# Laying a scan group's pieces inside the next group's projections in a hybrid attention and state-space layer

## The chip, the cores and the metric

The kernel runs on one NeuronCore of one Trainium2 chip. The metric is the device time of one execution in microseconds (us); lower is better. TensorE does the matrix products and transposes, VectorE (DVE in the profile), ScalarE (ACT) and GpSimd (POOL) the elementwise work, and SyncE (SP) issues all DMAs in one queue, in order.

## The reference, cut to what matters

One layer over 512 latent tokens and 256 context tokens, width 2048. The normalised input goes through one combined projection `w_in`, whose columns feed a windowed attention (q, k, v, a gate) and a bidirectional state-space scan in 4 groups of 4 heads (x, B, C, two step sizes dt, a gate z). The scan of a group, for each direction and in chunks of 128 tokens:

```python
    a_cs = jnp.cumsum(a_t, axis=-1)
    cb = jnp.einsum('bclgn,bcsgn->bgcls', cc, bc)
    wts = cb[:, :, None] * jnp.exp(segsum(a_t))
    y_diag = jnp.einsum('bgrcls,bcsgrp->bclgrp', wts, xdt)
    states = jnp.einsum('bclgn,bgrcl,bclgrp->bcgrpn', bc, decay_states, xdt)
    ...
    y_off = jnp.einsum('bclgn,bcgrpn,bgrcl->bclgrp', cc, prev, jnp.exp(a_cs))
    return (y_diag + y_off).reshape(b, l, g, r, p), final
```

x, B and C first pass a depthwise convolution of width 3 and a silu. The scan of the latent tokens starts from the context's final state; k, x and B are needed for context tokens too, q, C and the gates for latent tokens only. Both halves are then gated, normalised and sent through one output projection.

## The kernel before, in words

Every fp32 product of a projection is done as three products of a split operand (high and low part of the weight, `wh` and `wl`, and of the input, `xh` and `xl`, or `ch` and `cl` for the context). A **unit** is 128 projection columns: `load_unit` brings its weights in two DMAs (`wr`, 512 KB each, two buffers), ScalarE makes `wh` and VectorE makes `wl` in four quarters, and `proj` runs over 16 k blocks. For each it issues three products of 512 columns into the PSUM tile `pj` (L321 to L323) and, for units that the context needs, three products of 256 columns into `pjc` (L325 to L327). With every quarter `gate_step` (L274) adds one block of the residual gate's row in VectorE (L290), with a DMA `wg` each; after every 16 blocks it sums over the partitions in two TensorE instructions `gp` (L293).

The SSD stage takes 16 units, four for each group (two of x, one B, one C), and `ssd_group` (L474) writes them out group by group:

- four projections, each followed by `conv_silu` (L459), which reads the PSUM tiles three times each (L465, L466, L468);
- transposes of x and B into token layout (`xtp` L496, `btp` L503), copied by ScalarE into `xtok` and `btok`;
- the chunk states: `stc`, then three serial steps of `stx` for both directions, each with VectorE work (`xw`, `stt`) before and after;
- the product `cbp` of C and B, copied into `cb`;
- for each of two head pairs (`pr`): the state term `z` (L548); for each of four rows (2 heads, 2 directions) the **decay**: a broadcast DMA of the running sums into a tile `df` (L562, four buffers), exponentials on ScalarE, masks (L566), scaling (L573, L575) and the product with `cb` on VectorE; then the products `yps` (L586) of the pair's two decay matrices with `xtok`, the tile `yt` (L591) and three GpSimd instructions (sum of `ec`, `yt`, and the product into `yT`).

After the four groups the SSD pool is closed and the attention pool opens in the same room (`sst.close()`, L606; `at`, L610). The two key units (k0, k1) are projected in a loop there, each followed by its rotation `rope_apply` (L623, with the table `rp` loaded by a DMA at L620) into that pool. Then come `finish_half` of the scan's output, and four attention blocks whose query units (q0, q1 for the first) and gate units are projected in between.

The order on each engine is not the order of the text: a list scheduler, with a cost model of its own, takes the ready instruction of the best priority, which is the place in the text, moved forward in `high_priority` blocks. So products of the next units already fill gaps in a group's chain. What runs on the chip is then a fixed order for each engine, and a wait in it holds up all that is behind. PSUM has eight banks: 3 of tag `mm` (for `pj` and `pjc`), 2 `sa` (`z`), 2 `tp` (transposes, states, `cbp`, `gp`) and 1 `pv` (`yps`).

Of the kernel before, what the change touches and what calls it, by code (L numbers as in the profile page):

```python
# [14 lines left out]
P = 128  # L15
D = 2048
KT = 16
# [26 lines left out]
def emit(tc, xin, ctxT, wmod, wgate, bgate, wz, wvd, wu, wo, fng, vecs, cst, rope, out, dbg=None):  # L44
# [18 lines left out]
    with es:  # L63
# [24 lines left out]
        # persistent activations: transposed normalised inputs in two exact parts  # L88
# [27 lines left out]
        def rms_rows(o, acc, n, tag):  # L116
            """1 / rms of every token, on all partitions, from the sums of squares per partition."""
# [13 lines left out]
        def load_latent():  # L131
            """Latent tokens: transposed as they come, in column blocks; 1 / rms of every token on all partitions."""
# [44 lines left out]
        # silu of the two modulation vectors, zero-padded to one column group  # L177
# [95 lines left out]

        def gate_step(ld):  # L274
            """One k block of 512 gate columns: products per partition, summed over partitions after the last."""
# [3 lines left out]
            n, k = divmod(i, KT)  # L279
            if k == 0:  # L280
                ga = wp.tile([P, 512], F32, tag="ga", name=f"ga_{n}", bufs=1)
# [9 lines left out]
            if k == KT - 1:  # L291
                gp = bank("tp", f"gp_{n}", shape=(1, 512))
                mm(gp, ones[:, 0:1], ga, True, True)  # L293
                nc.scalar.activation(ga[0:1, :], gp, AF.Copy)
                nc.sync.dma_start(grow[:, n * 512:(n + 1) * 512], ga[0:1, :])

# [1 line left out]
        def load_unit(u, ctxp=False):  # L298
            """Yields (k, hi, lo) weight blocks [128, 128] of unit u."""
# [16 lines left out]
        def proj(u, with_ctx):  # L316
            a = bank("mm", f"pj_{u}")
            b = bank("mm", f"pjc_{u}", shape=(P, CT)) if with_ctx else None
            for k, wh, wl in load_unit(u):
                s0, s1 = k == 0, k == KT - 1  # L320
                mm(a, wh, xh[k], s0, False)  # L321
                mm(a, wh, xl[k], False, False)
                mm(a, wl, xh[k], False, s1)  # L323
                if with_ctx:
                    mm(b, wh, ch[k], s0, False)  # L325
                    mm(b, wh, cl[k], False, False)
                    mm(b, wl, ch[k], False, s1)  # L327
            return a, b

# [80 lines left out]
        # dt: softplus(u) = max(u,0) + log1p(exp(-|u|)), log1p(e) = 2 atanh(e / (2 + e))  # L410
        fl = [P, 192]
        uu = dtt.rearrange("p a b c -> p (a b c)")
        ue = w2("ue", "sm", 4, fl)
        us = w2("us", "sm", 4, fl)
        u2 = w2("u2", "sm", 4, fl)
        acc = w2("acc", "sm", 4, fl)
# [12 lines left out]
        da = w2("da", "sm", 4, fl)  # L429
# [13 lines left out]
        dd = w2("dd", "sm", 4, fl)  # L443
# [6 lines left out]
        csx = w2("csx", "sm", 4, [P, NT, 2, 16])  # L450
# [8 lines left out]
        def conv_silu(pa, pb, ci, o):  # L459
            """Depthwise conv of width 3 and silu: pa [128, n] in PSUM -> o in SBUF."""  # L460
# [13 lines left out]
        def ssd_group(g, units):  # L474
            ux0, ux1, ub, uc = units
            xs = []
            for i, u in enumerate((ux0, ux1)):
# [532 lines left out]
```

## Time and profile before

| what | value |
|---|---|
| device time, three executions | 1060.71, 1056.16 and 1057.65 us, median 1057.65 |
| profiled execution, span from first to last instruction | 1054.8 us |
| TensorE (PE) busy | 1009.6 us, 96% |
| TensorE weight loads (PEld) busy | 818.7 us, 78% |
| VectorE (DVE) busy | 722.0 us, 68% |
| ScalarE (ACT) busy | 494.6 us, 47% |
| GpSimd (POOL) busy | 173.5 us, 16% |
| mean granted TensorE clock | 0.989 of full speed |

The span is 2.85 us below the median of the three times. A busy share is the time in which an engine had an instruction open; for TensorE, whose matmuls overlap, a busy engine is not one at its peak.

### The profile page before, as it was taken

The numbers are of one execution on the slowest core, as the hardware profiler recorded it, in microseconds if no ns is written. First come the engines' busy times: TensorE is split into PE (matmuls) and PEld (weight loads), VectorE is DVE, ScalarE is ACT, GpSimd is POOL, SyncE is SP. The second block draws the span as 40 slices with busy tenths as digits, with TensorE's granted clock in tenths as the row PEclk, the third lists the DMA queues.
The fourth block names the chain that finished last, engine by engine and source line by source line (L and its number), as shares of the span: only waits on it lengthen the run. The fifth ranks groups of instructions, "written<-read, shape, count | busy, mean of one in ns | idle before, by whom it ended". The sixth has DMA issues, their size and how long they took to land.

```text
span 1054.8 us, 15524 instructions
## 1 busy us (share of the span) xinstructions
PE 1009.6 (96%) x5682; PEld 818.7 (78%) x5682; DVE 722.0 (68%) x1474; ACT 494.6 (47%) x1064; POOL 173.5 (16%) x120
## 2 busy tenths in 40 slices
PE   5999999999999989989989999999999998999996
PEld 4677789788778868868868777777777777888885
DVE  4332378585875985885889888788798866333765
ACT  6222275263352453263345567666666655333333
POOL 1232200000210110110037100000000008744220
PEclk9999999999999999989999999999999999999998
DMA  9999963354244244444331211112111135442304
GB/s 333 385 347 348 343 212 95 110 165 147 70 120 145 92 149 125 112 120 139 120 107 56 84 61 42 59 40 80 41 40 61 61 99 221 151 167 91 100 33 160
DMA packets 50845, 143.25 MB, mean 136 GB/s; under 512 B 5544, under 2 KB 5928, under 8 KB 50512
## 3 DMA queue, kind: packets, MB, share of 16 engines
q1 hardware_dynamic: 50768, 142.25, 40.5%
q8 instruction: 45, 0.74, 0.3%
q14 instruction: 32, 0.26, 0.1%
HBM read 137.96 MB, written 4.27 MB: 135 GB/s over the span
## 4 chain that ended last, share of the span: by engine, by line
PE 61%; DVE 12%; DMA 5%; ACT 3%; issue 3%; POOL 1%; SPq 0%; ACTq 0%; DVEq 0%; POOLq 0%
PE pj L49 25%; PE o L49 14%; PE pjc L49 5%; PE pv L49 3%; PE ptp L756 3%; PE sl L49 3%; DMA wg<-in_wgate_dram 2%; PE vps L49 2%; DVE df L566 2%; DVE wl L55 2%; DMA df<-csd 2%; PE sc L49 2%; DVE ga L290 1%; DVE df L575 1%; PE stx L49 1%
## 5 line engine op out<-in xcount | busy, mean ns | idle before, releaser
L49 PE MATMUL pj<-xh,wh 128*128 128x512 f32 x560 | 225.5, 403 | 0.0
L49 PE MATMUL pj<-xl,wh 128*128 128x512 f32 x560 | 224.6, 401 | 0.0
L49 PE MATMUL pj<-xh,wl 128*128 128x512 f32 x560 | 224.0, 400 | 0.0
L308 ACT ACTIVATE wh<-wr 128x512 fp32r<-128x512 f32 x140 | 87.9, 630 | 137.5 <-PE pjc L49 66.2
L49 PEld LDWEIGHTS pj<-xh,wl 128*128 128x128 f32 x560 | 105.7, 189 | 21.3 <-issue 0.9
L55 DVE TENSOR_TENSOR wl<-wr,wh 128x512 fp32r<-128x512 f32 x140 | 103.5, 742 | 24.9 <-ACT wh L308 21.0
L49 PEld LDWEIGHTS pj<-xl,wh 128*128 128x128 f32 x560 | 106.4, 190 | 15.1 <-issue 1.9
L49 PEld LDWEIGHTS pj<-xh,wh 128*128 128x128 f32 x560 | 106.5, 190 | 13.9 <-issue 1.0
L55 DVE TENSOR_TENSOR wol<-wo,woh 128x512 fp32r<-128x512 f32 x56 | 53.3, 968 | 63.6 <-ACT woh L846 57.3
L290 DVE SCALAR_TENSOR_TENSOR ga<-wg,sc,ga 128x512 f32<-128x512 f32 x64 | 50.8, 794 | 49.2 <-DMA wg<-in_wgate_dram 48.1
L55 POOL TENSOR_TENSOR ec<-ec,ec 128x512 f32<-128x512 f32 x8 | 11.2, 1397 | 349.2 <-DVE ec L55 328.9
L846 ACT ACTIVATE woh<-wo 128x512 fp32r<-128x512 f32 x56 | 34.8, 630 | 70.8 <-PE o L49 62.3
L55 POOL TENSOR_TENSOR hacc<-hacc,hsq 128x512 f32<-128x512 f32 x14 | 20.4, 1454 | 288.7 <-ACT hsq L654 286.3
L49 PE MATMUL pjc<-chq,wh 128*128 128x256 f32 x224 | 65.2, 291 | 2.1 <-DVE xs L468 2.1
L49 PE MATMUL pjc<-clq,wh 128*128 128x256 f32 x224 | 64.4, 288 | 0.0
L49 PE MATMUL pjc<-chq,wl 128*128 128x256 f32 x224 | 63.7, 284 | 0.0
L760 ACT ACTIVATE ph<-ptp 128x512 fp32r<-128x512 f32 x72 | 41.1, 597 | 28.2 <-PE ptp L756 26.8
L49 PE MATMUL o<-woh,hsh 128*128 128x512 f32 x128 | 50.9, 397 | 3.1 <-ACT part L865 3.1
L55 DVE TENSOR_TENSOR pl<-ptp,ph 128x512 fp32r<-128x512 f32 x72 | 48.4, 683 | 7.8 <-ACT ph L760 7.4
L566 DVE SCALAR_TENSOR_TENSOR df<-df,cs,cs_sb 128x128 f32<-128x128 f32 x128 | 48.3, 433 | 4.6 <-ACT ec L563 4.5
L49 PEld LDWEIGHTS pjc<-chq,wh 128*128 128x128 f32 x224 | 42.2, 189 | 11.5 <-ACT ec L563 1.6
L55 POOL TENSOR_TENSOR wsl<-wsr,wsh 128x896 fp32r<-128x896 f32 x16 | 33.9, 2116 | 101.0 <-ACT wsh L231 95.7
(282 smaller groups left out, 2341.8 us busy)
## 6 DMA issues: line engine op xcount, KB each, us to landing
wr<-in_wu_dram SPq DMA_DIRECT2D x70, 512.0 KB, 3.9
wm<-in_wmod_dram SPq DMA_DIRECT2D x64, 512.0 KB, 7.5
wg<-in_wgate_dram SPq DMA_DIRECT2D x64, 256.0 KB, 2.6
wo<-in_wo_dram SPq DMA_DIRECT2D x32, 512.0 KB, 4.5
df<-csd SPq DMA_DIRECT2D x32, 256.0 KB, 4.1
wsr<-in_wz_dram SPq DMA_DIRECT2D x16, 448.0 KB, 6.6
wr_v<-in_wvd_dram SPq DMA_DIRECT2D x16, 288.0 KB, 2.9
xt<-in_xin_dram SPq DMA_DIRECT2D x8, 512.0 KB, 7.5
```

Source lines behind the costliest of these rows:

```text
L49: return nc.tensor.matmul(o, l, r, start=start, stop=stop)
L55: eng.tensor_tensor(out=o, in0=a, in1=b, op=op)
L290: geng.scalar_tensor_tensor(out=ga, in0=wg, scalar=sc0[:, k:k + 1], in1=ga, op0=ALU.mult, op1=ALU.add)
L308: nc.scalar.activation(wh, rr, AF.Copy)
L566: nc.vector.scalar_tensor_tensor(out=df[:, cc], in0=bc[:, cc], scalar=cs[:, d, c, r:r + 1], in1=mF if d == 0 else mB, op0=ALU.subtract, op ...
L575: nc.vector.scalar_tensor_tensor(out=dx[0][:, cc], in0=df[:, cc], scalar=dtt[:, d, c, r:r + 1], in1=dx[0][:, cc], op0=ALU.mult, op1=ALU.add)
L756: nc.tensor.transpose(tp[:, i * P:(i + 1) * P], pt[i][:, n * P:(n + 1) * P], ident)
L760: nc.scalar.activation(ph, tp, AF.Copy)
L846: nc.scalar.activation(wh, wr[:, i, :], AF.Copy)
```

## The change

Four things are edited.

1. `ssd_group` is taken apart into functions (`stream`, `tokens`, `states`, `decay`, `state_term`, `back`), and `proj` gets an argument `mid`, a table from a k block to a function that is written out ahead of that block. The pieces of group g are so written inside the four units of group g + 1; those of the last group inside k0 and k1, which move ahead of the close of the SSD pool and keep their PSUM tiles until the rotation. `pjc` of k1 goes to a `tp` bank.
2. The three context products of a k block are no longer issued right behind its latent products, but four blocks together at the end of each quarter.
3. The `gp` sum of the gate's row is issued three gate steps later (after the last row, behind the last group), with a second buffer for `ga`.
4. Room: the x and B tiles get four slots handed out by name in place of three of one tag, and the small tiles of the step sizes share the `df` buffers.

```diff
+        def gate_sum():
+            while gpend:
+                n = gpend.pop()
...
+                mm(gp, ones[:, 0:1], ga, True, True)
...
+            if k == 3:
+                gate_sum()
...
-        def proj(u, with_ctx):
+        def proj(u, with_ctx, mid=(), btag="mm"):
             a = bank("mm", f"pj_{u}")
-            b = bank("mm", f"pjc_{u}", shape=(P, CT)) if with_ctx else None
+            b = bank(btag, f"pjc_{u}", shape=(P, CT)) if with_ctx else None
+            late = []
             for k, wh, wl in load_unit(u):
                 s0, s1 = k == 0, k == KT - 1
+                if k in mid:
+                    mid[k]()
                 mm(a, wh, xh[k], s0, False)
                 mm(a, wh, xl[k], False, False)
                 mm(a, wl, xh[k], False, s1)
                 if with_ctx:
-                    mm(b, wh, ch[k], s0, False)
-                    mm(b, wh, cl[k], False, False)
-                    mm(b, wl, ch[k], False, s1)
+                    late.append((k, wh, wl))
+                    if k % 4 == 3:
+                        for kk, h, l in late:
+                            mm(b, h, ch[kk], kk == 0, False)
+                            mm(b, h, cl[kk], False, False)
+                            mm(b, l, ch[kk], False, kk == KT - 1)
+                        late = []
...
+        def small(name, n=192):
+            return w2(name, "df", DF)[:, 0:n]
...
+        slots = ["xs0", "xs1", "xs2", "xs3"]
+        G = [{} for _ in range(4)]
+
+        def stream(g, i, mid=()):
...
+            a, b = proj(u, i < 3, mid)
...
+            conv_silu(a, b, (2 * g, 2 * g + 1, 8 + g, 12 + g)[i], o)
...
+        def tokens(g):
...
+            cbp = bank("tp", f"cbp_{g}")
...
+            slots.append(G[g]["slot2"])
+
+        def states(g):
...
+        def decay(g, pr):
...
+        def state_term(g, pr, tags=("sa", "sa")):
...
+            for d in range(2):
+                tt(nc.vector, ecs[d], zs[d], ecs[d], ALU.mult)
+            tt(nc.gpsimd, ecs[0], ecs[0], ecs[1], ALU.add)
+
+        def back(g, pr):
...
+            yps = bank("pv", f"yps_{tix}")
...
+        for i in range(4):
+            stream(0, i)
+        kps = []
         for g in range(4):
-            ssd_group(g, [U0 + 4 * g + i for i in range(4)])
...
+            if g < 3:
+                stream(g + 1, 0, {8: tok})
+                sta()
+                stream(g + 1, 1, {4: dec[0], 8: ste[0]})
+                stream(g + 1, 2, {8: do(bck[0], dec[1], ste[1])})
+                stream(g + 1, 3, {8: bck[1]})
+            else:
+                kps.append(proj(U0 + 16, True, {8: tok, 12: sta}))
+                dec[0]()
+                kps.append(proj(U0 + 17, True, {4: do(ste[0], dec[1]), 10: bck[0], 14: ste[1]}, "tp"))
+                bck[1]()
+        gate_sum()
...
-            a, b = proj(U0 + 16 + i, True)
+            a, b = kps[i]
```

`tokens` holds `cbp`, `xtp` and `btp` with their copies; `states` the `stc` and `stx` steps; `decay(g, pr)` the four rows of one head pair; `state_term` the `z` products and the three instructions on `ec`; `back` the `yps` products and what follows them. Their bodies are those of `ssd_group`; the order within is as before except that `cbp` comes first.

## Rows read from the trace of the kernel before

**Rows 1.** Busy time by stage; times in us from the span's start, instructions in brackets.
```profile
core 0: us, PE busy (x) PEld busy (x) DVE busy (x) ACT busy (x) POOL busy (x), PEclk, DMA share, GB/s
195.30:260.30 65.00, 62.63 (x344) 53.67 (x343) 45.83 (x99) 28.15 (x53) 0.00 (x0) 1.00 0.49 153
260.30:343.30 83.00, 78.82 (x450) 66.31 (x449) 61.39 (x125) 35.55 (x69) 8.46 (x7) 0.98 0.37 113
343.30:426.50 83.20, 78.34 (x458) 66.06 (x457) 63.96 (x129) 36.55 (x70) 8.53 (x7) 1.00 0.41 124
426.50:509.50 83.00, 78.45 (x441) 65.47 (x440) 63.78 (x130) 34.57 (x68) 8.58 (x7) 0.96 0.44 127
509.50:564.30 54.80, 50.81 (x305) 41.87 (x304) 47.34 (x87) 23.45 (x44) 14.46 (x10) 0.97 0.29 90
592.00:866.00 274.00, 273.47 (x1452) 215.03 (x1451) 225.43 (x545) 170.15 (x446) 0.00 (x0) 1.00 0.17 54
```

**Rows 2.** Waits of TensorE, 183 to 592: who waited for whom, us, times, longest.
```profile
PE yps L49 <- DVE df L55: 13.6, 4, 4.0
PE pjc L49 <- DVE xs L468: 2.1, 2, 1.2
PE gp L49 <- DVE ga L290: 1.9, 1, 1.9
```

**Rows 3.** Timeline of TensorE in a unit: start, us, instruction.
```profile
299.37 0.39 PE L49 MATMUL pj<-xl,wh 128*128 128x512 f32 x1
299.60 0.40 PE L49 MATMUL pj<-xh,wl 128*128 128x512 f32 x1
...
301.38 0.28 PE L49 MATMUL pjc<-clq,wh 128*128 128x256 f32 x1
301.50 0.28 PE L49 MATMUL pjc<-chq,wl 128*128 128x256 f32 x1
```

**Rows 4.** Timeline of TensorE in the first group's own products.
```profile
265.95 1.13 PE L49 MATMUL stc<-xw,btok 128*128 128x256 f32 x4
...
273.42 2.33 PE L49 MATMUL z<-cT,stt 128*128 128x128 f32 x18
275.50 0.48 PE L49 MATMUL pj<-xl,wh 128*128 128x512 f32 x1
...
276.15 1.09 PE L49 MATMUL yps<-df,xtok 128*64 128x128 f32 x16
277.17 0.38 PE L49 MATMUL z<-cT,stt 128*128 128x128 f32 x1
```

**Rows 5.** Timeline of TensorE at the last group's end; idle before in brackets.
```profile
526.71 1.09 PE L49 MATMUL yps<-df,xtok 128*64 128x128 f32 x16
...
543.43 1.45 PE L49 MATMUL yps<-df,xtok 128*64 128x128 f32 x16 [3.95 <-DVE df L55]
...
545.41 0.63 PE L49 MATMUL pj<-xh,wh 128*128 128x512 f32 x1
...
564.31 0.39 PE L49 MATMUL pj<-xh,wh 128*128 128x512 f32 x1
```

**Rows 6.** Timeline of VectorE and GpSimd: masks of the decay, and one GpSimd instruction.
```profile
285.70 1.14 DVE L566 SCALAR_TENSOR_TENSOR df<-df,cs,cs_sb 128x128 f32<-128x128 f32 x4
...
445.88 3.32 DVE L566 SCALAR_TENSOR_TENSOR df<-df,cs,cs_sb 128x128 f32<-128x128 f32 x4
...
446.13 1.29 POOL L55 TENSOR_TENSOR yt<-yt,ec 128x512 f32<-128x512 f32 x1 [1.38 <-DVE yt L591]
```

**Rows 7.** DMA issues, 195 to 560: count, KB each, median us to landing.
```profile
df<-csd SPq DMA_DIRECT2D x32, 256.0 KB, 4.1
rp<-in_rope_dram SPq DMA_DIRECT2D x1, 512.0 KB, 5.1
```

**Rows 8.** Timeline of VectorE: the rotation's two reads of k0's PSUM tile.
```profile
553.64 0.69 DVE L55 TENSOR_TENSOR kr<-pj,rp 128x512 f32<-128x512 f32 x1 [0.41 <-DMA rp<-in_rope_dram]
...
555.30 0.74 DVE L625 STREAM_SHUFFLE krt<-pj 128x512 f32<-128x512 f32 x1
```

More of the change, by code (lines that the diff above doesn't have):

```diff
@@ L531, in ssd_group @@
                     tt(nc.vector, stt_[d][:, nx, :], stt_[d][:, nx, :], sp_, ALU.add)
-            cbp = bank("tp", f"cbp_{g}")
+            G[g]["stt"] = stt_
+        def decay(g, pr):
+            cb = G[g]["cb"]
+            tix = 2 * g + pr
+            ecs = [w2(f"ec_{tix}_{d}", "ec", 3) for d in range(2)]
+            dm = []
+            for hh in range(2):
+                r = tix * 2 + hh
+                hr = slice(hh * 64, hh * 64 + 64)
+                dx = []
+                for d in range(2):
+                    df = w2(f"df_{r}_{d}", "df", DF)
+                    bc = df
+                    with tc.high_priority(HB):
+                        nc.sync.dma_start(df, csd[d * 16 + r].partition_broadcast(P))
+                    nc.scalar.activation(ecs[d][hr], bc[hr], AF.Exp)
+                    for c in range(NT):
+                        cc = slice(c * P, (c + 1) * P)
+                        nc.vector.scalar_tensor_tensor(
+                            out=df[:, cc], in0=bc[:, cc], scalar=cs[:, d, c, r:r + 1],
+                            in1=mF if d == 0 else mB, op0=ALU.subtract, op1=ALU.min)
+                    nc.scalar.activation(df, df, AF.Exp)
+                    for c in range(NT):
+                        cc = slice(c * P, (c + 1) * P)
+                        if d == 0:
+                            nc.scalar.activation(df[:, cc], df[:, cc], AF.Copy, scale=dtt[:, d, c, r:r + 1])
+                        else:
+                            nc.vector.scalar_tensor_tensor(out=dx[0][:, cc], in0=df[:, cc],
+                                                           scalar=dtt[:, d, c, r:r + 1], in1=dx[0][:, cc],
+                                                           op0=ALU.mult, op1=ALU.add)
+                    dx.append(df)
+                tt(nc.vector, dx[0], dx[0], cb, ALU.mult)
+                dm.append(dx[0])
+            G[g]["dec", pr] = dm, ecs
@@ new lines, in state_term @@
+        def state_term(g, pr, tags=("sa", "sa")):
+            stt_, cT = G[g]["stt"], G[g][3]
+            ecs = G[g]["dec", pr][1]
+            tix = 2 * g + pr
+            zs = []
+            for d in range(2):
+                z = bank(tags[d], f"z_{tix}_{d}")
+                for c in range(NT):
+                    cc = slice(c * P, (c + 1) * P)
+                    mm(z[:, cc], stt_[d][:, c, pr * P:(pr + 1) * P], cT[:, cc], True, True)
+                zs.append(z)
+            for d in range(2):
+                tt(nc.vector, ecs[d], zs[d], ecs[d], ALU.mult)
+            tt(nc.gpsimd, ecs[0], ecs[0], ecs[1], ALU.add)
@@ L597, in emit @@
[L597 to L599 removed]
+                for hh in (1, 0):
+                    hl = pr * 2 + hh
+                    mmo(yps[hh * 64:hh * 64 + 64, cc], xtok[:, c, hl * HD:hl * HD + HD], dm[hh][:, cc], True, True)
+            yt = w2(f"yt_{tix}", "cve", 1)
+            nc.vector.scalar_tensor_tensor(out=yt, in0=xs[:, 0:S], scalar=dskh[:, tix:tix + 1], in1=yps,
+                                           op0=ALU.mult, op1=ALU.add)
@@ new lines, in back, with do @@
+            tt(nc.gpsimd, yt, yt, ec, ALU.add)
+            tt(nc.gpsimd, yT[tix], yT[tix], yt, ALU.mult)
+            slots.append(G[g][f"slot{pr}"])
+        for i in range(4):
+            stream(0, i)
+        kps = []
+        for g in range(4):
+            def do(*fs):
+                return lambda: [f() for f in fs]
+            tok, sta = (lambda: tokens(g)), (lambda: states(g))
+            dec = [lambda pr=pr: decay(g, pr) for pr in range(2)]
+            ste = [lambda pr=pr: state_term(g, pr) for pr in range(2)]
+            bck = [lambda pr=pr: back(g, pr) for pr in range(2)]
+            if g < 3:
[4 more added lines that the diff above has]
+                stream(g + 1, 3, {8: bck[1]})
+            else:
+                kps.append(proj(U0 + 16, True, {8: tok, 12: sta}))
+                dec[0]()
+                kps.append(proj(U0 + 17, True, {4: do(ste[0], dec[1]), 10: bck[0], 14: ste[1]}, "tp"))
+                bck[1]()
```

116 lines of the change are left out of this document (33 added, 83 removed).

## The prediction

> **What bounds the kernel now.** I read the stages first [rows 1], then what TensorE waits for in the SSD stage [rows 2], then the timeline around the longest of these waits [rows 5] and around the instructions that end it [rows 6].
>
> TensorE is the bound. In the attention stage it is busy for 273.5 of 274 us, so nothing can be won there, only lost. The SSD stage is looser: group 0's units take 65.0 us with 2.4 idle, the three stretches that each hold one group's tail and the next group's units take 83.0, 83.2 and 83.0 us with 4.2, 4.9 and 4.5 idle (length less PE busy), and the last, with k0, k1 and group 3's tail, 54.8 us with 4.0 idle [rows 1]. VectorE is busy for 61 to 64 us of a period (74 to 77%): loaded, but not the bound.
>
> The idle time has an owner. Of what TensorE waits for there, 13.6 us in four waits is `yps` on the `df` tile, one in each group; 2.1 us is `pjc` on the convolution that still reads its PSUM bank, and 1.9 us is one `gp` on its last gate step [rows 2]. The four are the second head pair's. In the last group `yps` of pair 0 starts at 526.71 and that of pair 1 at 543.43, 16.7 us later, with TensorE idle for the last 3.95 [rows 5]: the decay of pair 1 takes longer than the products that lie under it. Behind that wait the next 512-column product takes 0.63 us instead of 0.39 [rows 5, 3], and the granted clock of the stretches with such waits is 0.98, 1.00, 0.96 and 0.97, where the others have 1.00 [rows 1]: part of the time at 1.2 instead of 2.4 GHz.
>
> **How much there is to win.** Back to back, a 512-column product is issued every 0.23 us (299.37 to 299.60) and a 256-column one every 0.12 [rows 3]. A group's four units have 192 and 144 of them: 192 x 0.23 + 144 x 0.12 = 44.2 + 17.3 = 61.5 us. The group's own products, counted from the loops (an fp32 product shows as two instructions): 58 of `z`, `cbp`, `xtp`, `btp` at (275.50 - 273.42) / 18 = 0.116 each make 6.7 us; 32 `yps` at (277.17 - 276.15) / 16 = 0.064 make 2.0; 20 `stc` and `stx` at no more than 1.13 / 4 = 0.28 make 5.6 [rows 4]; two `gp`, taken as two 512-column products each, 1.0. Sum 15.3. So a period needs 61.5 + 15.3 = 76.8 us of TensorE and takes (83.0 + 83.2 + 83.0) / 3 = 83.1: 6.3 us are lost, of which 4.5 is idle and 1.8 the slow clock and the mixing of short and long products. Over three periods at most 18.8 us can come back. The last stretch needs 96 x 0.23 + 96 x 0.12 + 15.3 = 48.9 us and takes 54.8 [rows 1]: 5.9 lost.
>
> **The change part by part.** Nothing is removed or added in work: the same products, DMAs (`df` 32, `rp` 1 [rows 7]), ScalarE and VectorE instructions. What moves is where they stand.
>
> *Group tails inside the next units, three periods.* Between the last product of C's unit and the pieces that need its convolution lie 8 k blocks, 8 x (0.69 + 0.36) = 8.4 us. Pair 0's decay now has all of unit 1 from block 4 on and half of unit 2: 12 x 1.05 + 8.4 = 21 us, more than the 16.7 of a decay between two `yps`; its wait, zero before, stays zero. Between the two `back` pieces lie half of unit 2 (8.4), the `z` products (16 x 0.116 = 1.9) and half of unit 3, which has no context products (8 x 0.69 = 5.5): 15.8 us against a chain of 16.7. So of each 3.4 us (13.6 / 4) about 0.9 stays; with a wait that short I expect no slow clock. Of the 1.8 us of mixing I leave 0.4, since the state steps still alternate with unit 1's products. Left over 1.3 a period, so won 3 x (6.3 - 1.3) = 15.0 us. Bounds: nothing (the chain grows by as much as its cover) to 18.8.
>
> *A rule against it.* The chain of 16.7 us is partly GpSimd's doing: four masks of the decay took 3.32 us while GpSimd worked on `yt`, and 1.14 us elsewhere [rows 6]. In the change `decay` of pair 1 still stands right behind `back` of pair 0, which issues those GpSimd instructions, so I keep the longer duration; by the shorter one the chain would be 2.2 us less, and the 0.9 left would go too, 2.7 us in three periods. The Trainium skill ("SBUF — State Buffer", section "Who interferes with whom") says why: a VectorE instruction with two SBUF inputs and a GpSimd one that reads SBUF exclude each other through a shared port. The trace agrees (3.32 against 1.14 us).
>
> *Context products a quarter behind.* Their rate is the same in a batch of 12 as elsewhere (0.12 us [rows 3]); cost nothing. A unit's `pj` is now complete 12 x 0.12 = 1.4 us before the unit ends, so the convolution starts that much earlier, and the next unit needs its second bank only after 12 latent products, 2.8 us. The two waits of at most 1.2 us [rows 2] go: 1.2 of the 2.1 lies in the periods and is in the sum above; the other 0.9, in group 0, is extra. If VectorE is late with the convolution they come back, 2.1 at most.
>
> *The `gp` sum three gate steps later.* Its 1.9 us wait [rows 2] lies in a period, already counted. *Shared small tiles, four slots, second `ga`*: nothing; the step sizes are done before the first `df` is wanted, and each slot is freed at least half a unit ahead of its next writer. Cover gone: a wait of the convolution for one `yt`.
>
> *SP's queue.* The `df` DMAs, some of which wait for a buffer that `yps` frees, move past weight loads; the weights queue behind them. TensorE has no wait on `wl` in this stage [rows 2], since a weight buffer holds half a unit (8.4 us). Hidden as long as an SP wait stays below that; each us beyond is a us on TensorE.
>
> *The last group.* Before, k1 lay behind group 3's end and filled the time until the rotations had freed PSUM banks: after `yps` came the rest of k0 and all of k1, and q0 began at 564.31 without a wait [rows 5]. Now k0 and k1 are used up as cover. Two waits can appear. First, pair 1's decay starts 6 k blocks (6.3 us) before `back` of pair 0, whose `df` buffers it needs for its last row; behind that `back` lie 6 x 1.05 + 1.9 = 8.2 us of products. The chain of 16.7 less 6.3 is 10.4: a wait of 2.2 us. It is 0 if only the last row is left (its DMA 4.1 and masks 1.14 fit [rows 6, 7]), 8.5 if the whole chain is. Second, k0's two tiles and k1's hold all three `mm` banks when q0 wants one. The first to go is k0's context tile, one ScalarE copy; I take 1.5 us, which the last `gp` partly covers. If that copy's room is not free, q0 waits for the rotation: the table's DMA of 5.1 us [rows 7] and two reads of 0.69 and 0.74 [rows 8], 6.5 us. With the same 2 us of slow clock and mixing as before: 48.9 + 2.2 + 1.5 + 2.0 = 54.6 against 54.8. So 0.2 won, which I count as nothing; bounds +5.9 and 48.9 + 8.5 + 6.5 + 2.0 = 65.9, a loss of 11.
>
> **Sum.** 15.0 + 0.9 + 0 = 15.9 us off the span of 1054.8, so 1038.9. The median of the runs is 2.85 above the span, so 1041.7; I say 1042.
>
> **Rivals.**
> - *All of it comes back*: no wait in any period, and the last stretch at its floor. 18.8 + 2.4 (group 0's idle) + 5.9 = 27 us: 1031. For it: the cover is only 0.9 us short of the chain, and the masks' short duration would close that. Against: the last stretch has less cover, not more.
> - *The chain stays the pace*: VectorE has the same 61 to 64 us to do in a shorter period, in order; decays that start later than before, behind convolutions and states, arrive as late as now. Each period keeps 3.4 us of wait and its clock, and only `pjc` (2.1), `gp` (1.9) and some mixing come back, some 5 us: 1053, no change to speak of. For it: the chain's hand-overs between DMA, ScalarE and VectorE are untouched. Against: pair 0 never waited, with a cover like the one pair 1 now gets.
> - *Slower: the end is bare.* Place: between k1's last product and q0's first. TensorE has nothing else to issue there, so wait for the chain (8.5) and for the rotation (6.5) are both paid, 11 us lost; behind it VectorE has both rotations and `finish_half` to do, which k1 used to cover: the two reads and two more instructions of each rotation, at about 0.7 each [rows 8], are 5.6 us that q2 may wait for, and the slow clock some 3 more. 20 us lost against 15.9 won: 1062. It decides from a bare end of 16 us on. For it: all three `mm` banks are in use. Against: both waits must be at their upper end.
> - *The planner undoes it*: the scheduler orders by its own costs, so the pieces land about where they were: 1057, within 3.
>
> **How the numbers follow.** Forecast (1035 to 1049) 0.53; all of it (below 1035) 0.17; the chain stays 0.14; undone 0.05; slower 0.11. The range leaves out about 0.07 below and 0.12 above: 1031 to 1058. 0.5% of 1057.65, about what a measurement here can tell from no change, is 5.3 us: faster means below 1052.4. Forecast, all of it and half of "the chain stays" are faster: 0.77. The other half and "undone" are the same: 0.12. Slower 0.11.
>
> **What would show it.** Right: waits of `yps` on `df` below 4 us together, none of `pjc` on a convolution, none of `gp`; the three periods near 78 us between C units; granted clock 0.99 or more in them; one idle stretch of 2 to 4 us before q0's first `pj`. Wrong: `yps` waits as large as now (the chain sets the pace), a new wait of `pj` on `wl` (SP's queue held up), idle time of over 10 us at the end of k1, or an attention stage longer than 274 us.

## The result, and the profile after

The changed kernel takes 1070.76 us in the median of four executions (1070.01 to 1073.7) against 1058.44 of the kernel before beside it: a ratio of 1.0121, 95% interval 1.0098 to 1.0144. It is 12 us slower where 16 us faster were forecast, outside the range of 1031 to 1058.

Below, a unit's end is the start of its last 512-column product, and the stages are cut there: the end of group 0's C unit, the three periods from one C unit's end to the next, and from the last one to q0's first product, to the first score product `sl`, to the last `pj`, and to the end. Busy time by stage of the kernel after, columns as in [rows 1]:

```profile
core 0: us, PE busy (x) PEld busy (x) DVE busy (x) ACT busy (x) POOL busy (x), PEclk, DMA share, GB/s
195.00:261.90 66.90, 63.70 (x341) 54.37 (x340) 46.05 (x100) 27.71 (x52) 0.00 (x0) 0.97 0.50 150
261.90:340.30 78.40, 77.14 (x450) 65.03 (x449) 55.19 (x112) 28.96 (x53) 6.90 (x6) 1.00 0.37 114
340.30:422.90 82.60, 78.53 (x449) 66.23 (x448) 59.85 (x129) 35.40 (x68) 8.34 (x7) 0.98 0.41 126
422.90:508.20 85.30, 80.61 (x449) 67.87 (x449) 60.80 (x131) 35.60 (x68) 8.89 (x7) 0.94 0.40 125
508.20:567.70 59.50, 51.37 (x307) 43.18 (x305) 35.53 (x83) 23.24 (x48) 7.75 (x6) 0.94 0.24 78
567.70:601.40 33.70, 27.47 (x97) 21.07 (x97) 30.38 (x38) 16.19 (x29) 25.56 (x17) 0.85 0.19 60
601.40:878.50 277.10, 275.48 (x1464) 216.74 (x1465) 229.33 (x554) 171.47 (x451) 0.00 (x0) 1.00 0.17 56
```

The same view of the kernel before, for the two stretches that [rows 1] cuts elsewhere:

```profile
509.30:564.30 55.00, 51.01 (x306) 42.00 (x305) 47.34 (x87) 23.46 (x44) 14.46 (x10) 0.97 0.29 90
564.30:586.70 22.40, 22.40 (x98) 18.04 (x97) 22.17 (x23) 10.26 (x19) 17.40 (x11) 1.00 0.22 71
```

The ledger of the two profiled executions (spans 1054.8 and 1071.7 us; the one of the kernel after is the slowest of its four, so they differ by 16.9 us where the medians differ by 12.3): to the end of group 0's C unit 260.1 became 261.9 (+1.9, forecast -0.9); the three periods 249.2 became 246.3 (-2.9, where -15.0 was forecast); C's end to q0 55.0 became 59.5 (+4.5, forecast -0.2); q0 to the first `sl` 22.4 became 33.7 (+11.3, no term in the forecast's sum; 6.2 of it idle time of TensorE, 5.1 longer busy time at a granted clock of 0.85 instead of 1.00); then +0.8 and +1.4. The first period is the forecast's 78; the second and third are not, and their granted clock is 0.98 and 0.94.

What TensorE waits for, 183 to 640 us, after, to be read beside [rows 2]:

```profile
PE xtp L528 <- ACT cb L520: 9.0, 3, 3.4
PE pj L49 <- DVE wl L55: 5.4, 2, 3.4
PE cbp L49 <- DVE cT L110: 4.4, 3, 2.2
PE pjc L49 <- ACT df L593: 3.2, 1, 3.2
PE yps L49 <- DVE df L55: 3.0, 1, 3.0
```

The waits that were to go did go: `yps` fell from 13.6 us in four to 3.0 in one, which is the last group's, and `gp` is gone. But `xtp` and `cbp`, which never waited, now wait 13.4 us in six: the new loss stands at the first pieces of groups 1 to 3 (8.8 us in the second and third period, 4.6 behind the last C unit). In group 0's own units `pjc` waits 3.2 us for ScalarE. ScalarE's and TensorE's timeline at group 1's tokens shows who is late (start, us; idle before in brackets):

```profile
341.52 0.63 ACT L587 ACTIVATE ec<-df 64x512 f32<-64x512 f32 x1 [4.26 <-DMA df<-csd]
...
345.44 0.78 ACT L485 ACTIVATE cT<-pj,v_sb 128x512 f32<-128x512 f32 x1
...
348.38 0.63 ACT L109 ACTIVATE cve<-cT 128x512 f32<-128x512 f32 x1
...
349.84 1.16 PE L49 MATMUL cbp<-cT,xs 128*128 128x128 f32 x8 [0.71 <-DVE cT L110]
...
353.86 0.63 ACT L593 ACTIVATE df<-df 128x512 f32<-128x512 f32 x1 [2.63 <-DVE df L590]
354.39 0.58 ACT L520 ACTIVATE cb<-cbp 128x512 f32<-128x512 f32 x1
...
355.03 0.66 PE L528 MATMUL xtp<-c_sb,xs 128*128 128x128 f32 x4 [3.36 <-ACT cb L520]
```

C's last product began at 340.28, but the first read of its convolution is issued at 345.44, behind an exponential of the decay for which ScalarE stood 4.26 us (its row was still in flight). `cbp` runs at 349.84, and its copy `cb` at 354.39, behind another exponential that stood 2.63 us for VectorE's masks. The decay is not urgent at that place: `ec` is wanted with `z`, which starts at 379.5, a unit and a half later, and `df` with the pair's `yps` at 399.4.

At the attention's start the waits of `pj` on `wl` show a second loss. VectorE, GpSimd and TensorE there:

```profile
587.57 1.51 DVE L723 TENSOR_SCALAR hfu<-y,v_sb 128x512 f32<-128x512 f32 x1
589.01 1.75 DVE L55 TENSOR_TENSOR kr<-kr,krt 128x512 f32<-128x512 f32 x1
590.17 1.71 POOL L55 TENSOR_TENSOR hsl<-hfu,hsh 128x512 fp32r<-128x512 f32 x1
590.68 1.75 DVE L55 TENSOR_TENSOR wl<-wr,wh 128x512 fp32r<-128x512 f32 x1
...
592.48 0.80 PE L49 MATMUL pj<-xh,wl 128*128 128x512 f32 x1 [3.40 <-DVE wl L55]
...
593.91 0.47 DVE L723 TENSOR_SCALAR hfu<-y,v_sb 128x512 f32<-128x512 f32 x1
...
599.76 0.68 DVE L55 TENSOR_TENSOR wl<-wr,wh 128x512 fp32r<-128x512 f32 x1
```

VectorE is busy for 30.4 of these 33.7 us (22.2 of 22.4 before) with rotations, the norm's gain (`hfu`) and weight parts, many of them at 1.5 to 1.8 us while GpSimd works on the same norm (25.6 us busy, 17.4 before). `wl` comes in its turn, TensorE stands, and the product behind the wait takes 0.80 us instead of 0.39.

### The profile page after: what moved, and what is told of

It is laid out like the page before. It is cut to its first block, busy times and chain, and to the rows that moved or that the text cites. A ratio compares the mean times of both kernels' runs of the same rounds, so it can differ in the third digit from the quotient of the medians.

```text
span 1071.7 us, 15525 instructions
## 1 busy us (share of the span) xinstructions
PE 1018.7 (95%) x5682; PEld 826.6 (77%) x5682; DVE 707.6 (66%) x1474; ACT 494.4 (46%) x1064; POOL 175.0 (16%) x120
## 4 chain that ended last, share of the span: by engine, by line
PE 71%; DVE 10%; DMA 9%; ACT 5%; issue 3%; POOL 1%; SPq 0%; ACTq 0%; DVEq 0%; POOLq 0%
PE pj L49 23%; PE o L49 14%; PE zps L49 7%; DMA df<-csd 4%; DMA wg<-in_wgate_dram 4%; PE pjc L49 4%; PE vps L49 4%; PE md L49 3%; PE pv L49 3%; PE ptp L822 3%; PE sl L49 3%; PE sc L49 2%; DVE df L590 1%; DVE wl L55 1%; DVE ga L303 1%
## 5 line engine op out<-in xcount | busy, mean ns | idle before, releaser
L49 PE MATMUL pj<-xh,wl 128*128 128x512 f32 x560 | 228.3, 408 | 5.4 <-DVE wl L55 5.4
L49 PE MATMUL pj<-xh,wh 128*128 128x512 f32 x560 | 231.7, 414 | 0.5 <-ACT kT L702 0.5
L49 PE MATMUL pj<-xl,wh 128*128 128x512 f32 x560 | 227.4, 406 | 0.0
L55 DVE TENSOR_TENSOR wl<-wr,wh 128x512 fp32r<-128x512 f32 x140 | 97.3, 696 | 36.6 <-ACT wh L318 35.8
L303 DVE SCALAR_TENSOR_TENSOR ga<-wg,sc,ga 128x512 f32<-128x512 f32 x64 | 48.3, 755 | 35.2 <-DMA wg<-in_wgate_dram 35.0
L49 PE MATMUL pjc<-chq,wh 128*128 128x256 f32 x224 | 63.6, 284 | 3.2 <-ACT df L593 3.2
L49 PE MATMUL pjc<-clq,wh 128*128 128x256 f32 x224 | 63.6, 284 | 0.0
L590 DVE SCALAR_TENSOR_TENSOR df<-df,cs,cs_sb 128x128 f32<-128x128 f32 x128 | 38.9, 347 | 28.9 <-ACT ec L587 28.9
L587 ACT ACTIVATE ec<-df 64x512 f32<-64x512 f32 x32 | 20.1, 629 | 72.2 <-DMA df<-csd 55.0
L49 PE MATMUL o<-wol,hsh 128*128 128x512 f32 x128 | 50.8, 397 | 0.0
```

The costliest lines, as they stand in the source:

```text
L49: return nc.tensor.matmul(o, l, r, start=start, stop=stop)
L55: eng.tensor_tensor(out=o, in0=a, in1=b, op=op)
L303: geng.scalar_tensor_tensor(out=ga, in0=wg, scalar=sc0[:, k:k + 1], in1=ga, op0=ALU.mult, op1=ALU.add)
L587: nc.scalar.activation(ecs[d][hr], bc[hr], AF.Exp)
L590: nc.vector.scalar_tensor_tensor(out=df[:, cc], in0=bc[:, cc], scalar=cs[:, d, c, r:r + 1], in1=mF if d == 0 else mB, op0=ALU.subtract, op ...
```

## Experiments

All runs in one table. Ratios are to the kernel before on the same chip, with the interval in brackets; the stages are of the one profiled execution each, cut as above. "Period" is the mean of the three, "C to sl" runs from the last C unit's end to the first `sl`, "output" from the last `pj` ahead of the output projection to the end.

| kernel | us | ratio | period | C to sl | sl to last pj | output |
|---|---|---|---|---|---|---|
| before | 1058.4 | 1 | 83.1 | 77.4 | 276.3 | 191.8 |
| after | 1070.8 | 1.0121 [1.0098, 1.0144] | 82.1 | 93.1 | 277.1 | 193.2 |
| e1 k0, k1 written behind | 1071.8 | 1.0125 [1.0100, 1.0149] | 82.4 | 93.1 | 278.4 | 193.3 |
| e2 decay's rows held on SP | 1075.2 | 1.0158 [1.0126, 1.0189] | 82.2 | 95.2 | 277.1 | 193.3 |
| e3 norm a block later | 1071.4 | 1.0119 [1.0085, 1.0152] | 82.1 | 83.0 | 286.5 | 194.3 |
| e5 after, context inline | 1073.0 | 1.0141 [1.0119, 1.0163] | 82.5 | 93.4 | 277.0 | 193.3 |
| e4 before, context batched | 1054.2 | 0.9974 [0.9953, 0.9995] | 82.4 | 76.6 | 276.3 | 191.7 |
| e6 decay behind the tokens | 1052.7 | 0.9956 [0.9939, 0.9973] | 78.3 | 86.9 | 277.2 | 193.3 |
| e7 end as before | 1061.6 | 1.0041 [1.0023, 1.0059] | 81.5 | 84.4 | 276.1 | 192.3 |
| e8 = e6 + e7 | 1051.8 | 0.9953 [0.9936, 0.9969] | 77.3 | 87.7 | 277.0 | 193.3 |
| e9 = e8, last group not held | 1049.7 | 0.9935 [0.9921, 0.9950] | 78.0 | 85.9 | 276.8 | 193.6 |
| e10 = e6 + gain on ScalarE | 1046.2 | 0.9893 [0.9874, 0.9913] | 78.7 | 83.0 | 278.6 | 188.8 |
| e11 before, batch and late gp | 1061.9 | 1.0044 [1.0028, 1.0061] | 84.4 | 79.0 | 276.2 | 194.5 |
| e12 = e9 + gain on ScalarE | 1044.0 | 0.9881 [0.9866, 0.9896] | 78.1 | 82.9 | 277.2 | 188.9 |
| e13 = e12, cbp late in group 3 | 1044.1 | 0.9869 [0.9845, 0.9893] | 78.2 | 86.3 | 276.9 | 188.4 |
| e14 after, cbp last everywhere | 1071.0 | 1.0140 [1.0104, 1.0176] | 82.2 | 92.8 | 277.2 | 193.2 |
| e15 = e13, all four held | 1045.5 | 0.9868 [0.9839, 0.9897] | 78.0 | 86.6 | 277.2 | 189.2 |

### First guesses: the end's order, the rows' DMA, the norm, the batch

**e1.** k0 and k1 are written behind the last group's pieces, but still ahead of the close of the SSD pool.

```diff
-                kps.append(proj(U0 + 16, True, {8: tok, 12: sta}))
-                dec[0]()
-                kps.append(proj(U0 + 17, True, {4: do(ste[0], dec[1]), 10: bck[0], 14: ste[1]}, "tp"))
-                bck[1]()
+                tok()
+                sta()
+                for pr in range(2):
+                    dec[pr]()
+                    ste[pr]()
+                    bck[pr]()
+                kps.append(proj(U0 + 16, True))
+                kps.append(proj(U0 + 17, True, (), "tp"))
```

> The changed kernel with k0 and k1 written behind the last group's pieces instead of around them; all else as changed. Theory A (k1 was the cover under which VectorE did the rotations and the scan's norm, and without it TensorE waits for weight parts at the attention's start): from the last SSD product on it is as before, the waits of q0 and q1 on the weight parts (5.4 us) and the slow clock behind them go, and the time falls by 8 to 13 us, to 1058 to 1063. Theory B (the decay, pulled ahead by the planner, stands in ScalarE's queue waiting for its DMA, with convolutions and copies behind it): the periods stay as they are in the changed kernel, cbp and xtp still wait some 10 us, and B's part of the loss is still there. Rival C (the batching of the context products is what costs): no change here, 1070.

No gain: C to `sl` stays at 93.1 us. Two stretches of e1, the first while k0 and k1 run and the second behind it, show why this is not the order of the kernel before, where each rotation is written right behind its unit; here both stand behind both units.

```profile
549.00:576.40 27.40, 26.46 (x132) 21.65 (x129) 7.90 (x14) 7.44 (x14) 9.82 (x8) 0.91 0.24 77
576.40:603.80 27.40, 20.71 (x78) 15.27 (x77) 26.86 (x39) 14.48 (x28) 14.38 (x10) 0.90 0.18 58
```

VectorE is busy 7.9 of 27.4 us, then 26.9 of the next 27.4. A unit covers only what may run beside it.

**e2.** The decay's rows are held on SP's queue behind the last issued weight load.

```diff
+        lastld = []
...
+                    lastld[:] = [ld]
...
-                    with tc.high_priority(HB):
+                    with tc.high_priority(HB), tc.issue_after(lastld[0].ins):
                         nc.sync.dma_start(df, csd[d * 16 + r].partition_broadcast(P))
```

> The changed kernel with each decay's DMA tied behind the last weight load written before it, so that the planner can't pull a group's decay into the units ahead of its place. Theory B: ScalarE's waits on the df DMA fall from 55 us to under 25, the waits of cbp and xtp (13.4 us) and the wait of pjc (3.2) fall below 4 us together, periods come to 78 to 80 us, and the time falls by 8 to 14 us, to 1057 to 1063, with the attention's start as slow as in the changed kernel. Theory A alone: no change, 1070. Against both: the decay now comes too late and yps waits in each group, 1075 or more.

Missed: the wait at the tokens grew to 17.1 us (the line below and 2.1 of `cbp`; 13.4 in after).

```profile
PE xtp L531 <- ACT cb L523: 15.0, 4, 4.2
```

ScalarE's own waits for the rows did not fall either (53.8 us, 55.0 in after). Holding a row on SP does not change what ScalarE has in its queue ahead of the copy.

**e3.** The norm of the SSD output (`finish_half`, ScalarE, VectorE and GpSimd) is written behind the first attention block instead of ahead of it.

```diff
-        s_hi, s_lo, s_acc = finish_half(lambda t: yT[t], ...)
...
             if j == 1:
+                s_hi, s_lo, s_acc = finish_half(lambda t: yT[t], ...)
                 half_rstd(s_acc, 1)
```

> The changed kernel with the norm of the scan's output (finish_half, 15 GpSimd instructions and 8 of VectorE) written behind the first attention block instead of ahead of it. Theory A with GpSimd's part in it (VectorE's two-input instructions take 1.5 to 1.8 us instead of 0.7 beside GpSimd): weight parts, rotations and masks at the attention's start take 0.7 us again, TensorE's waits there (about 8 us with the slow clock behind them) go, and the time falls by 6 to 12 us, to 1059 to 1065. If the lost cover alone matters and not GpSimd's share: 1 to 4 us. If the work only moves and blocks VectorE in the second block instead, 1070 again.

q0 to the first `sl` of e3, and the stretches of the second block where the norm then runs:

```profile
565.40:588.70 23.30, 23.25 (x97) 18.72 (x98) 17.27 (x32) 9.10 (x16) 2.96 (x2) 0.96 0.35 116
...
642.00:668.00 26.00, 22.63 (x103) 16.78 (x101) 23.03 (x41) 18.40 (x39) 15.24 (x11) 0.93 0.07 23
668.00:694.00 26.00, 22.04 (x115) 17.95 (x115) 18.80 (x44) 16.01 (x41) 6.91 (x5) 0.93 0.18 63
```

Without the norm the stretch is 23.3 us, near the 22.4 of before and 10.4 below after. The attention then pays 286.5 - 277.1 = 9.4 us for it in the second block. So the norm costs TensorE some 10 us in either place. In the kernel before it began beside k1 (first `hfu` at 547.6 us, q0 at 564.3), and what was left ran beside q0 and q1, with TensorE busy for 22.40 of 22.4 us.

**e5** and **e4** take the context batch out of the changed kernel, and put it alone into the kernel before (e5's edit is shown, e4's is its reverse).

```diff
-                    late.append((k, wh, wl))
-                    if k % 4 == 3:
-                        ...
+                    mm(b, wh, ch[k], s0, False)
+                    mm(b, wh, cl[k], False, False)
+                    mm(b, wl, ch[k], False, s1)
```

> The changed kernel with the context products back right behind the latent ones of their k block. Theories A and B: the batch is not the cause; 1068 to 1074, with up to 3 us more of pjc waiting on convolutions. Rival C (the batch is what costs, since a convolution that is late by ScalarE's queue meets twelve products in one go): 1060 or less.

> The kernel before with one part of the change: context products a quarter unit behind. If that part is worth what the prediction gave it (the waits of pjc on the convolution, 2.1 us, mostly go), 1055.5 to 1058, no difference to tell. Rival: holding four weight blocks of a quarter until its end makes the weight copies late; then waits of pj on wl of some us appear and the time is above 1063.

Neither moves the time by much: e5's interval overlaps that of after, e4 is 0.05 to 0.5% below before. The batch is not the cause of the loss.

### The order on ScalarE

**e6.** One edge: the first ScalarE read of each decay row goes behind the group's last token copy, on ScalarE's own queue. No data and no other engine is waited for.

```diff
...
-                    nc.scalar.activation(ecs[d][hr], bc[hr], AF.Exp)
+                    with tc.issue_after(G[g]["copied"].ins):
+                        nc.scalar.activation(ecs[d][hr], bc[hr], AF.Exp)
```

(`copied` is the second `btok` copy.)

> The changed kernel, with the first ScalarE read of each decay row (L587) put behind the group's last token copy on ScalarE's own queue. Theory A (the periods lose because the planner puts pair 0's decay ahead of the convolution of C and of the copies cb and xtok, and ScalarE stands there in order): the waits of cbp and xtp, 13.4 us in six, fall below 4, the three periods are 79 to 80.5 us instead of 82.7, 84.2 and 84.2, and the whole is 1059 to 1064. Rival (VectorE's work is the pace: what isn't waited for at the copies is waited for at the decay): cbp and xtp fall, but yps goes from 3 back to 10 or more, and the time stays within 3 us of 1071.

It hit, and by more than expected: 1052.7 us, 18 below after. The same stages of e6, from the end of group 0's C unit to the first `sl`:

```profile
258.20:335.30 77.10, 77.08 (x449) 65.00 (x448) 60.73 (x128) 35.27 (x68) 8.60 (x7) 1.00 0.42 130
335.30:414.00 78.70, 77.53 (x450) 64.97 (x449) 61.81 (x132) 35.20 (x68) 7.93 (x7) 1.00 0.43 132
414.00:493.10 79.10, 77.68 (x450) 65.07 (x449) 61.89 (x130) 35.25 (x68) 8.89 (x7) 1.00 0.42 134
493.10:548.60 55.50, 50.58 (x306) 41.61 (x305) 38.84 (x95) 25.78 (x55) 7.00 (x7) 0.97 0.25 79
548.60:580.00 31.40, 24.73 (x96) 18.92 (x96) 29.98 (x37) 16.12 (x29) 23.93 (x16) 0.95 0.18 55
```

TensorE idles 2.6 us in three periods, the granted clock is 1.00, and the periods come to 77.1, 78.7 and 79.1: 14.3 us won, where the forecast had 15.0. ScalarE at group 1's tokens, where it had stood for decays:

```profile
345.11 0.60 ACT L520 ACTIVATE cb<-cbp 128x512 f32<-128x512 f32 x1 [0.38 <-PE cbp L49]
...
347.79 0.88 ACT L536 ACTIVATE btok<-btp 128x512 f32<-128x512 f32 x2 [0.26 <-PE btp L535]
348.55 2.32 ACT L588 ACTIVATE ec<-df 64x512 f32<-64x512 f32 x4
```

The copies follow their products within half a microsecond, and the four exponentials come behind them without a wait. The rival, that the wait would come back at `yps`, fell: `yps` waits once in e6, 4.0 us, in the last group.

**e14** asks whether `cbp` standing first among the products (its copy holds one of two `tp` banks) would explain the waits instead. Changed kernel, decay not held, `cbp` and `cb` behind `btp` in every group.

> The changed kernel with one edit: in every group cbp comes behind the transposes, the decay isn't held. If the wait at the tokens is an effect of cbp standing first (its copy holds one of two tp banks), the waits of cbp and xtp, 13.4 us, go, and the time is 1058 to 1062. If it is ScalarE's queue (the token copies behind the exponentials of the decay, whichever product is first), the waits only move to the third transposes or to btp: 1068 to 1074.

```profile
PE xtp L532 <- ACT xtok L534: 15.6, 3, 5.7
```

1071.0 us: the wait only moves to the third transposes, which need the bank of the first. With e6 that makes ScalarE's order the cause, and not the product's place.

### The end

**e7** puts the last group as it was: the pieces one behind the other, the SSD pool closed, then k0 and k1 in the attention's loop with each rotation right behind its unit (and the gate's last sum behind k0, with the `ga` buffers handed out to match). **e8** is e6 and e7 together.

```diff
-                kps.append(proj(U0 + 16, True, {8: tok, 12: sta}))
...
+                tok()
+                sta()
+                for pr in range(2):
+                    dec[pr]()
+                    ste[pr]()
+                    bck[pr]()
...
-            a, b = kps[i]
+            a, b = proj(U0 + 16 + i, True)
+            gate_sum()
```

> The changed kernel with the last group as in the kernel before: its pieces one behind the other, then k0 and k1, each with its rotation right behind it. Theory B (with k0 and k1 used up as cover, rotations and the norm of the SSD output meet the first queries bare; 12.1 us more from q0's first to the last unit's last product, and 3.4 us before it): the first sl comes 10 to 14 us earlier than 601.4 and the whole is 1056 to 1061. Rival (the norm of the SSD output costs the attention stage its time wherever it lies, as when it was moved behind the first block): the time stays within 4 us of 1071, with the loss moved to another block.

> The two edits of the decay put behind the token copies and of the last group as before together. If the two losses are separate, the gains add: 1044 to 1052, below the kernel before. If both are one shortage of VectorE time, the sum is no more than 3 us better than the better of the two alone.

e7 is 0.8% below after (1061.6 us, 0.6 above the expected range; its profiled execution, the fastest of ten, took 1057.6). C to `sl` is 84.4 us, 8.7 shorter, and all of that lies behind q0 (columns as above):

```profile
564.00:587.50 23.50, 22.65 (x99) 17.94 (x98) 23.21 (x23) 10.46 (x19) 17.55 (x12) 1.00 0.21 68
```

From q0 to the first `sl` e7 takes 23.5 us, where after takes 33.7 and before 22.4: with k0 and k1 given back as cover, the second loss is all but gone. C's end to q0 is no shorter (60.9 against 59.5). But the gains don't add: e8 is the same as e6, with C to `sl` 87.7 against 86.9. With the decay held, k0 and k1 behind the pieces buy nothing: the waits of `wl` shrink from 4.8 to 2.7 us, and 2.7 of `cbp` on C's convolution come in their place.

**e9** holds the decay only in groups 0 to 2 (`G[min(g, 2)]` in e6's edge), on e8.

> As the run with both edits (1051.8 us), but the last group's decay isn't held behind its token copies. Theory C (the hold is right where units follow and wrong in the last group: from C's end to the first sl VectorE has 65 to 73 us of work, 69.5 of 76.4 in the kernel before, and held decays leave it idle at the start of that stretch): that stretch falls from 87.7 to 77 to 80 us and the whole to 1041 to 1045, the time predicted for the change. Rival (what is lost there isn't the hold but the convolution of C behind decays, as in the run with the end alone undone, 84.4 us): 1048 to 1052.

2 us came, not 8, and the intervals of e8 and e9 overlap: C to `sl` is 85.9. `cbp` stands 5.9 us for the convolution, which again has exponentials ahead of it.

**e10** and **e12** put the eight multiplications by the norm gain on ScalarE, on e6 and on e9. The edit acts in both calls of the norm, the second of them between attention and output projection.

```diff
-                    nc.vector.tensor_scalar(out=full, in0=y, scalar1=vec(goff, t), scalar2=None, op0=ALU.mult)
+                    nc.scalar.activation(full, y, AF.Copy, scale=vec(goff, t))
```

> As the run with the decay behind the token copies (1052.7 us), but the eight multiplications by the norm gain (L724, 0.48 us each, 1.5 us beside GpSimd) are on ScalarE instead of VectorE. Theory D (behind the last yps VectorE is the pace: 30 of 31.4 us busy from 548.6 to 580.0, its two-input instructions 1.75 us instead of 0.68 beside GpSimd's norm): the waits of pj on wl, 4.8 us, go to under 1, and the whole to 1044 to 1049. Rival (the two-input instructions just stretch over GpSimd's time, whatever else VectorE has): within 2.5 us of 1052.7.

> The first two of these together: the decay held in groups 0 to 2 alone, the end as in the kernel before, the gain multiplications on ScalarE. If VectorE is still the pace behind the last yps with k0 and k1 there, 3 to 5 us below the run without the gain edit; if k0 and k1 are cover enough, the same within 2.5 us.

Both gained: 0.6% and 0.5%. The ledger says where: C to `sl` is 4.0 and 3.0 us shorter, the output part 4.5 and 4.7. In e10 the waits on `wl` are gone, and the first `sl` waits instead:

```profile
PE sl L49 <- DVE qs L55: 5.4, 1, 5.4
```

So VectorE is the pace there, but some of what it no longer does ahead of `wl` is only waited for at `qs`; more than half of the gain lies in the second norm, of which the expectation had not thought.

**e13** moves `cbp` behind the transposes and state steps in the last group, on e12. **e15** also holds the decay there.

> As the run with the hold in three groups, the end undone and the gain on ScalarE (1044.0 us), but in the last group the product cbp, which alone needs C's convolution, comes behind the transposes and state steps, as in the kernel before. Theory E (with k0 and k1 behind the pieces again, what is left of the end's loss is TensorE standing 5.3 us at cbp for the convolution of C): the stretch from C's end to the first sl falls from 82.9 to 77 to 79 us, and the whole to 1038 to 1041. Rival (VectorE is full there anyway, so the wait only moves): 1042 to 1046.

> As the run before with cbp late in the last group (1044.1 us), but the decay held behind the token copies in all four groups. In that run TensorE stood 5.6 us at the last transposes, while ScalarE stood 3.58 us for a mask and 3.02 us for a decay row ahead of C's convolution and of the copies xtok. If it is this order that costs, the 5.6 us go, C's end to the first sl is 77 to 80 us instead of 86, and the whole is 1037 to 1041. If VectorE's load decides there (with the hold alone it was idle at the start of the stretch), the wait moves to yps and the time stays at 1042 to 1046.

Neither beats e12: 1044.1 and 1045.5 us. In e13 the 5.3 us of `cbp` moved to the last transposes (5.6 us), for ScalarE's order once more:

```profile
491.66 0.63 ACT L602 ACTIVATE df<-df 128x512 f32<-128x512 f32 x1 [3.58 <-DVE df L599]
495.31 0.63 ACT L596 ACTIVATE ec<-df 64x512 f32<-64x512 f32 x1 [3.02 <-DMA df<-csd]
...
498.47 0.76 ACT L487 ACTIVATE cT<-pj,v_sb 128x512 f32<-128x512 f32 x1
499.13 1.07 ACT L538 ACTIVATE xtok<-xtp 128x512 f32<-128x512 f32 x2
```

In e15 that wait is gone, and others stand in its place:

```profile
PE yps L49 <- DVE df L55: 3.6, 1, 3.6
PE stc L49 <- ACT btok L544: 3.1, 1, 3.1
PE sl L49 <- DVE qs L55: 2.6, 1, 2.6
```

**e11** is the kernel before with the small parts alone: the batch, the `gp` sum three gate steps later, and the tiles shared to make room.

> The kernel before with only the small parts of the change: context products a quarter unit behind, the gate sum three gate steps later, the small tiles shared so that a second sum tile has room. No piece of a group is moved. If the batch alone (1054.2 us) is held back by its 8.1 us of waits of gp on ga, these go and the time is 1045 to 1048. Rival (the wait moves on to yps, 2.9 us there, 13.6 before): 1052 to 1056.

In e4 `gp` had waited 8.1 us on `ga` while `yps` waited 2.9 instead of 13.6; in e11 `gp` doesn't wait and `yps` is back.

```profile
PE gp L49 <- DVE ga L290: 8.1, 3, 2.7
PE yps L49 <- DVE df L55: 2.9, 1, 2.9
```
```profile
PE yps L49 <- DVE df L55: 15.3, 4, 4.1
```

(The first fence is e4, the second e11, whose profiled execution is 5.9 us above its median and is read for the waits alone.) So in the old arrangement the decay's chain looks like the pace: what TensorE stands for ahead of `yps` is taken off the wait there. The `yps` waits went for good only where the pieces were moved. This accounts for the waits and not for the whole time: e11 met neither of its ranges and is 0.3 to 0.6% slower than before, where e4 is faster. Which of the parts that e11 adds to e4 costs this, and why, is open.

## Why the prediction was wrong, point by point

- **What bounds the kernel, and how much a period can give: right.** 6.3 us lost in a period and some 78 us left were read off [rows 1 to 4]. e6 has 77.1, 78.7 and 79.1.
- **"Its wait, zero before, stays zero": right for `yps`, and wrong as a balance of the periods.** No `yps` waits in a period any more; the 0.9 us per period left for pair 1 was not even needed, so whether masks take 1.14 or 3.32 us [rows 6] decided nothing. The failed step is the sentence on what lies between C's last product and the pieces that need its convolution, "8 k blocks, 8 x (0.69 + 0.36) = 8.4 us". It counted cover in TensorE's products alone. On ScalarE the planner had put pair 0's exponentials between that product and the convolution and copies, and ScalarE takes them in order. That costs 13.4 us of waits and a clock down to 0.94, and the 0.9 us counted as won in group 0 became 1.9 lost; e6's edge brings 18 us back; of the 21.2 by which the profiled executions differ, 11.4 lie in the periods (246.3 to 234.9), 3.8 ahead of them and 6.2 behind (C to `sl` 93.1 to 86.9). That "the same products, DMAs" and "ScalarE and VectorE instructions" remain was said of their number; their order was not asked for.
- **"The planner undoes it" (0.05) named the right culprit with the wrong act.** It left the products where they were written and reordered the queue beside them.
- **The last group: C's end to q0 was right once the periods were.** Forecast 54.6 us, e6 55.5. The waits foreseen there came as 4.0 us (`yps`) and 0.9 (`pj` on the copy of k0's tile), for 2.2 and 1.5.
- **Behind it a term was missing from the sum.** "Now k0 and k1 are used up as cover" was followed by PSUM banks only. The rotations and the norm behind the last `yps`, 30.4 us of VectorE where 22.2 were left before, cost 11.3 us between q0 and the first `sl` in after, 9.0 in e6 (31.4 against 22.4), and 1.1 in e7, where k0 and k1 are cover again. The slower rival had this, at 5.6 us of VectorE and 3 of clock, 8.6 together, but tied it to two waits at their upper ends and gave it 0.11. e3 measures the norm's share at about 10 us, at the attention's start and in the second block alike.
- **Why VectorE is slow there.** `hfu` takes 1.51 us beside GpSimd and 0.47 alone (587.57 and 593.91 in after), a two-input instruction 1.75 and 0.68 (590.68 and 599.76). The Trainium skill ("SBUF — State Buffer", section "Who interferes with whom") has a rule for this: VectorE and GpSimd share a port pair that one of them holds for a whole instruction, for VectorE instructions with two SBUF inputs beside a GpSimd one that reads SBUF, and for `tensor_scalar` in its two-port modes. The rows agree, `hfu` included, which has one SBUF tensor. The multiplications by the gain, moved to ScalarE (e10, e12), are worth 0.5 to 0.6%. The prediction weighed this rule for the masks, where it did not matter, and not for the norm, where it did.
- **The batch, at "nothing" for its own cost and 0.9 us of gain: right in size.** e4 is 0.26% below before, 0.05 to 0.5% by its interval.
- **SP's queue, small tiles, four slots: no wait of theirs appears** on TensorE in the SSD stage, as said; the waits on `wl` lie behind it and are VectorE's. That the small tiles and the later `gp` cost nothing in time is not shown: e11, in the old arrangement, speaks against it.
- **The sum, term by term, with the first step put right.** From the span of 1054.8: -14.3 for the periods, -1.9 ahead of them (258.2 for 260.1), +9.5 for C to `sl`, +2.4 behind it give 1050.5, which is e6's span; the forecast had -15.0, -0.9, 0 and 0. Without the 9.5 at the end it would be 1041.0, some 1044 as a median by the forecast's 2.85: an estimate, which no run shows. The 2.4 behind the first `sl` was not followed up.

What stays open: in the versions with the periods right, C to `sl` is 83 to 88 us where the kernel before has 77.4. Where k0 and k1 are cover again, what is left lies ahead of q0: in e9, e12 and e13 C's end to q0 is 62.4, 59.6 and 63.6 us (before 55.0), q0 to `sl` 23.5, 23.3 and 22.7 (before 22.4). From e12 to e13 and e15 each edit there moved the wait (`cbp`, `xtp`, then `stc`, `yps` and `sl`) and left the time at 1044 to 1045.5. VectorE is busy 62 to 73 us of C to `sl` in these versions, 69.5 of 77.4 before; which order would give the 77 back was not found. Why e7's gain of 8.7 us at the end vanishes once the decay is held was not settled either: in e8 q0 to `sl` is 4.3 us shorter than in e6, and C's end to q0 5.1 longer.

The best version is e12 (e13 and e15 are no different): decay behind the token copies in groups 0 to 2, last group as before, the norm's gain on ScalarE. 1044.0 us, 0.9881 [0.9866, 0.9896] of the kernel before.

## What to carry to other kernels

When pieces of work are interleaved by hand on one engine, read the order that this gives on every other engine: an instruction that is merely early, on an engine that takes its queue in order, delays the urgent one behind it, and a single ordering edge can decide whether the whole move gains or loses (here 1070.8 or 1052.7 us, against 1058.4 before). When a unit is used as cover for one thing, ask what it covered until now, and find that work in the trace (here rotations and a norm, 9 to 11 us). A wait that is removed ahead of a chain that sets the pace can come back at the end of that chain, as `gp`'s did at `yps` between e4 and e11: see which of two waits is the chain's before pricing either.

## What the hardware showed that was not expected

A one-input `TENSOR_SCALAR` on VectorE was slowed as much as the two-input forms while GpSimd worked: 0.47 us alone, 1.51 beside it (0.68 and 1.75 for a two-input `TENSOR_TENSOR`). And idle time cost more than its own length: for about 450 TensorE instructions of a period the busy time itself is 77.1 us at a granted clock of 1.00 and 80.6 at 0.94, so the third period of after loses 4.7 us standing (85.3 less 80.6) and 2.9 more by running part of the time at 1.2 GHz (80.6 against 77.7 in e6).
